# A hybrid layer in split fp32 on one core: the first block's keys take the DRAM round trip that the later blocks' keys take

## The chip, the core and the metric

One core of a Trainium2 chip runs the whole program. Its engines work side by side, each through its own queue in order: TensorE (PE: matrix products into PSUM; PEld are its weight loads), VectorE (DVE), ScalarE (ACT) and GpSimd (POOL) for elementwise work, and SyncE (SP), which here only issues DMAs. GpSimd issues DMAs too. The metric is device time in microseconds (us) of one execution; lower is better.

## What is computed

One layer over 2048 prompt tokens and 64 sample tokens. One wide projection gives the inputs of two paths: a short convolution (path A) and a gated linear recurrence over 8 heads in chunks of 64 tokens (path B, HGRN2). The two are gated, merged, projected and normalised, and a last gate adds a per-layer embedding. The part that the change touches is the recurrence:

```python
def hgrn2_block(S, q, k, v, logf):
    b = jnp.cumsum(logf, axis=1)
    ref = b[:, (L - 1) // 2][:, None]
    qe = q * jnp.exp(b - ref)
    ke = k * jnp.exp(ref - b)
    att = jnp.where(causal, jnp.einsum('bthk,bshk->bhts', qe, ke), 0.0)
    o = jnp.einsum('bhts,bshv->bthv', att, v) + jnp.einsum('bthk,bhkv->bthv', q * jnp.exp(b), S)
    b_last = b[:, -1]
    S_new = jnp.exp(b_last)[..., None] * S + jnp.einsum('bshk,bshv->bhkv', k * jnp.exp(b_last[:, None] - b), v)
    return S_new, o
...
fg = lb + (1.0 - lb) * jax.nn.sigmoid(f)
logf = jnp.log(fg)
kk = 1.0 - fg
qq = jax.nn.silu(q) * QK_SCALE
S_new, o = hgrn2_scan(S0, qq, kk, vv, logf)
o = o * lax.rsqrt(jnp.mean(o * o, axis=-1, keepdims=True) + EPS)
```

The last product of `S_new` sums over tokens, so both keys and values must stand with tokens on the partitions for it, while everything before it has features there.

## The kernel before

**Tiling.** The 2112 tokens are cut into three blocks of 768, 704 and 640 (the 64 sample tokens lie in the second). Activations lie with 128 features on the partitions and the block's tokens in the free direction. Every large product is done with fp32 values split into a high and a low part (`hi`, `lo`; line 225), three matmuls for one, and most of them by a Strassen scheme: `sgroup` makes a group of two weight columns from seven products of half the size, each product being 12 matmuls (lines 445 to 447) of half a block's tokens. Weights come from DRAM through the buffers `raw`, `hi`, `lo` and `s`; all other tiles (`r`) share a ring of 48 buffers.

**Path B.** `path_b` runs over the 8 heads. `head_prep` makes a head's gates, keys and values with one group of seven products, and its queries and output gate with another; a call-back in the middle of that second group, `scaled`, makes the keys (`ka` for a pair's first chunk, `kb` with both chunks scaled to the pair's end; lines 1004 to 1013). In the first block a third group (`gates`) follows for each head but the first.

**Steps between products.** The attention of a head does not run at once. `path_b` puts its steps into numbered slots, and `sgroup` calls one slot after each product (`hook`), so that they run between the products of the next head. `head_attn` is a generator with a step at each `yield`: the product of queries and keys (L1122, L1124; `p_a`), the product of keys and values (L1137; `p_u`, from which the states follow on VectorE, L1152), the output (L1175, L1177; `p_o`), and in the first block a separate scaling. Each block has two such generators for a head (four groups of 128 tokens, then the rest). `turn_o`, `read_o` and `scale_o` then bring the head's output back to features on partitions, and it is stored (`o`).

**Getting tokens on the partitions.** `turned` lets VectorE transpose 32x32 blocks (L1064) into a staging tile and writes it to DRAM on GpSimd's queue (L1066); `in_rows` reads it back in another order, also on GpSimd's queue (L1071). For values (`tv`) and outputs (`to`) the result is used as it lands; for keys (`tk`), GpSimd copies it once more so that a group's columns lie side by side (L1076). Before the change the first block does this for values and outputs only: its keys are transposed by TensorE against an identity (L1104) into PSUM, and ScalarE copies them out (L1106). Blocks two and three do it for keys as well. There `head_prep` asks for the reads in the order values, the output of the head before, keys; the list is put together afterwards with the keys in front.

**What sets the order.** A tile scheduler sorts the instructions of each engine by the order in which the code emits them, by hints (`issue_after`, `high_priority`, `behind_all`), and by when it reckons an operand to be ready. What stands on one engine's queue then runs strictly in that order. On GpSimd's queue a DMA is only issued; the queue goes on to the next instruction while it travels. An instruction that needs data which have not landed holds the queue.

Of the kernel before, what the change touches and what calls it, by code (L numbers as in the profile page):

```python
# [18 lines left out]
P = 128  # L19
# [75 lines left out]
def hybrid_step(  # L95
# [66 lines left out]
    def ps_attn():  # L162
        return psa.tile([P, 512], F32, tag="pa", name=nm("pa"))
# [74 lines left out]
    lows, turn, stores = {}, [0], [SP]  # L238
# [700 lines left out]
    def head_prep(bl, hc, hd, first, hs, before):  # L939
        n, npair, turn = bl["n"], bl["npair"], bl["turn"]  # L940
        nch = n // CH
        odd_end = turn > npair
        sf, vt = rt(), rt(turn * P)
        if odd_end:
            V.memset(vt[:, n - CH : n], 0.0)

        def sink_f(c, h, x, y):
            if c == 0:
                A.activation(half(sf, h), whole(x, y), AF.Sigmoid)
                return  # L950
            n1 = 0
            if h == 0:
                n1 = 2 * SWAP * CH
                for odd in range(2):
                    c3, to = (slice(o, 2 * SWAP, 2) for o in (odd, 1 - odd))
                    into(chunks(vt)[:, to, :], chunks(x[:, :n1])[:, c3, :], None if y is None else chunks(y[:, :n1])[:, c3, :])
            n2 = hn() - CH * (h and odd_end)
            into(half(vt, h)[:, n1:n2], x[:, n1:n2], None if y is None else y[:, n1:n2])
            if n2 < hn():
                into(vt[:, n : n + CH], x[:, n2:], None if y is None else y[:, n2:])  # L960

        if hs and hd == 0:
            plain_group(FF * 8, IV * 8, hs, sink_f)
        else:
            sgroup(FF * 8 + hd, IV * 8 + hd, hc, sink_f, first)
        lg, staged_k, eq, staged_v = rt(), rt(turn * P), rt(), rt(turn * P)
        b, qx = staged_k[:, :n], staged_v[:, :n]
        wrote = [turned("tv", vt, staged_v, turn)]
        A.activation(lg, sf, AF.Ln, bias=lb[:, hd : hd + 1], scale=omlb[:, hd : hd + 1])
        if not first:  # L970
            V.tensor_scalar(sf, sf, nomlb[:, hd : hd + 1], omlb[:, hd : hd + 1], ALU.mult, ALU.add)
        V.tensor_tensor_scan(b, keep[:, :n], lg, 0.0, ALU.mult, ALU.add)
        ref = chunks(b)[:, :, CH // 2 - 1 : CH // 2]
        V.tensor_tensor(chunks(lg), chunks(b), ref.to_broadcast([P, nch, CH]), ALU.subtract)
        qc = small.tile([P, 2, BN // CH], F32, tag="qc", name=nm("qc"))
        f, r = qc[:, 0, :nch], qc[:, 1, :nch]
        ka, kb, qe, z = hf(turn * CH), rt(turn * P), rt(), rt()

        def scaled(after):


            with tc.issue_after(after):
                if first:
                    A.activation(sf, sf, AF.Identity, bias=omlb[:, hd : hd + 1], scale=nomlb[:, hd : hd + 1])
                A.activation(r, ref.rearrange("p c o -> p (c o)"), AF.Exp)
                A.activation(eq, lg, AF.Exp)
                A.activation(lg, lg, AF.Exp, scale=-1.0)
            V.tensor_tensor(f[:, 1:nch], r[:, 1:nch], chunks(eq)[:, : nch - 1, CH - 1], ALU.mult)
            V.tensor_copy(f[:, 0:1], r[:, 0:1])
            for g in bl["groups"]:  # L990
                if g["sample"]:
                    c = g["off"] // CH
                    V.tensor_copy(f[:, c : c + 1], r[:, c : c + 1])
            f1, f2 = f[:, 0 : 2 * npair : 2], f[:, 1 : 2 * npair : 2]

            ka3 = ka.rearrange("p (g t) -> p g t", t=CH)
            more = turn - 2 * SWAP
            for lo, hi, to in (
                (0, SWAP, ka3[:, more + 1 :: 2, :]),
                (SWAP, 2 * SWAP, ka3[:, more : turn - 1 : 2, :]),  # L1000
                (2 * SWAP, turn, ka3[:, :more, :]),
            ):
                own = slice(2 * lo, min(2 * hi, nch), 2)
                V.tensor_tensor(to, chunks(sf)[:, own, :], chunks(lg)[:, own, :], ALU.mult)
                hi = min(hi, npair)
                scale = f2[:, lo:hi].unsqueeze(2).to_broadcast([P, hi - lo, CH])
                place = slice(2 * lo + (hi <= SWAP), 2 * hi, 2)
                V.tensor_tensor(chunks(kb)[:, place, :], to[:, : hi - lo, :], scale, ALU.mult)
            if odd_end:
                V.tensor_copy(chunks(kb)[:, nch - 1 : nch + 1, :], ka3[:, more - 1 : more, :].to_broadcast([P, 2, CH]))  # L1010
            for lo, hi in ((0, SWAP), (SWAP, npair)):
                seconds, place = slice(2 * lo + 1, 2 * hi, 2), slice(2 * lo + (hi > SWAP), 2 * hi, 2)
                V.tensor_tensor(chunks(kb)[:, place, :], chunks(sf)[:, seconds, :], chunks(lg)[:, seconds, :], ALU.mult)
            if not first:
                wrote.append(turned("tk", kb, staged_k, turn))
            V.tensor_tensor(f2, f2, f1, ALU.mult)

        def queries():
            if first:
                A.activation(qe, qe, AF.Silu)  # L1020
                V.scalar_tensor_tensor(qe, qe, QK_SCALE, eq, ALU.mult, ALU.mult)
            else:
                sq = rt()
                A.activation(sq, qe, AF.Sigmoid)
                V.scalar_tensor_tensor(qe, qe, QK_SCALE, sq, ALU.mult, ALU.mult)
                V.tensor_tensor(qe, qe, eq, ALU.mult)
            V.tensor_tensor(chunks(qx), chunks(qe), f.unsqueeze(2).to_broadcast([P, nch, CH]), ALU.mult)

        def sink_q(c, h, x, y):
            if c == 1:  # L1030
                into(half(qe, h), x, y)
            elif first:
                A.activation(half(z, h), whole(x, y), AF.Silu)
                A.mul(half(z, h), half(z, h), g_on[:, hd : hd + 1])
            else:
                v = whole(x, y)
                A.activation(half(z, h), v, AF.Sigmoid)
                V.scalar_tensor_tensor(half(z, h), v, g_on[:, hd : hd + 1], half(z, h), ALU.mult, ALU.mult)  # L1038

        with behind_all(summed[-1] if first and hd == 0 else ()):  # L1040
            sgroup(ZB * 8 + hd, QQ * 8 + hd, hc, sink_q, first, mid=scaled, free=first)
        with tc.issue_after(freed[0]) if first else nullcontext():
            queries()
        with behind_all([*wrote, *powers]):
            by_token = [in_rows("tv", turn)]
            if before is not None and not first:
                before["ot"] = in_rows("to", turn, before["on"])
            if not first:
                by_token.insert(0, in_rows("tk", turn))
        return dict(  # L1050
            eq=eq, f=f, ka=ka, kb=kb, qe=qe, qx=qx, vt=vt, z=z, by_token=by_token, on=None,
            npair=npair, turn=turn, more=turn - 2 * SWAP, first=first, last=bl["last"], carry=None,
        )
# [6 lines left out]
    def turned(kind, src, out, npair):  # L1060

        n = npair * P
        blocks4 = out[:, :n].rearrange("p (j g a) -> p g j a", j=4, a=32)
        V.transpose(blocks4, src[:, :n].rearrange("p (g b j) -> p g j b", b=32, j=4))  # L1064
        turning[kind] = dram.tile([P, n], F32, tag=f"{kind}{npair}", name=nm(kind), bufs=2)
        return G.dma_start(turning[kind], out[:, :n]).ins  # L1066
# [12 lines left out]
    def head_attn(ip, gs, d, hd):  # L1079
# [16 lines left out]

        ready = [t[:, o0 // P : o0 // P + nt] for t in d["by_token"]]
        if len(ready) == 1:  # L1100
            turn_ = ps_attn()
            with placed():
                for i, g in enumerate(gs):
                    T.transpose(turn_[:, i * P : i * P + P], cols(d["kb"], g), ident)  # L1104
            ready.insert(0, tile3())
            A.copy(ready[0], cols3(turn_, nt))  # L1106
        kt, v = ready
        p_a = ps_attn()
        with placed():
            for i, g in enumerate(gs):  # L1110
# [105 lines left out]
    def path_b(bl, hc, first, kept, fills, hs, lead_sums=None):  # L1216
# [9 lines left out]
        for hd in range(NH):  # L1226
# [11 lines left out]
            if first:  # L1238
                late = int(hd == 0)
                for g in attn:  # L1240
                    for slot in (1 + late, 4, 7, 10):
                        at(slot + late + (g is attn[1]), g)
                at(13 + late, partial(turn_o, d))
                at(17 + late, partial(read_o, d))
                at(24 + late, partial(scale_o, d), keep)
                for slot in (15, 17, 19) if hd else (17,):
                    at(slot, piece)
                if hd == NH - 1:
# [539 lines left out]
```

## Time and profile before

| | us |
|---|---|
| median of 3 runs (lowest, highest) | 2538.24 (2536.97, 2540.58) |
| the profiled execution | 2538.01 |
| its span, first to last instruction | 2536.1 |

The core's granted clock is 1.00 over the span. The times of the stages can be read from the rows of path B: the heads of the first block run from some 60 to 500 us, those of the second from 1060 to 1345, those of the third from 1860 to 2130.

How the rows below are read: a group's row names line, engine, operation, `out<-in` tiles and count; a row in order of time starts with its start and duration in us, and ends, where the engine sat idle before it, with that idle time and what ended it. A row of waits says who waited for whom: total us, times, longest us. A row of stretches gives start and end, the length, then the busy us of PE, PEld, DVE, ACT and POOL, each with its count, then TensorE's granted clock, the DMA engines' busy share and GB/s.

### The profile page before, as it was taken

How to read it: one execution, taken by the hardware profiler on the slowest of the kernel's cores; microseconds unless marked ns; L12 is line 12 of the kernel's file. 1: busy time of each engine (PE TensorE's matmuls, PEld its weight loads, DVE VectorE, ACT ScalarE, POOL GpSimd, SP SyncE). 2: the span in 40 equal slices, each digit the busy share in tenths (PEclk: the TensorE clock that was granted, in tenths of full speed). 3: DMA queues.
4: the chain of work that ended last, by engine and by line, in shares of the span. 5: the costliest groups of instructions: out<-in, count | busy, mean ns of one | idle time of the engine just before them, and what ended most of it. 6: DMA issues, size and time to landing. Idle time of an engine off the chain costs nothing. (4 is left out here: it accounts for less than half of the span.)

```text
span 2536.1 us, 46699 instructions
## 1 busy us (share of the span) xinstructions
PE 2518.9 (99%) x15982; PEld 2506.1 (99%) x15982; DVE 1841.7 (73%) x3593; ACT 1495.8 (59%) x2916; POOL 455.1 (18%) x801
## 2 busy tenths in 40 slices
PE   9999999999999999999999999999999999999999
PEld 9999999999999999999999999999999999999998
DVE  7889888898868775477775657978357775446967
ACT  6766676654453764466655556567356664455675
POOL 2012121221022021122222311102212221001111
PEclk9999999999999999999999999999999999999999
DMA  8789888997697888889989988989989988789986
GB/s 332 244 293 334 308 302 304 331 333 268 231 346 246 270 287 315 278 298 318 307 295 310 339 303 304 329 280 313 330 304 317 324 296 283 254 258 314 335 273 202
DMA packets 356334, 755.02 MB, mean 298 GB/s; under 512 B 44214, under 2 KB 49520, under 8 KB 356096
## 3 DMA queue, kind: packets, MB, share of 16 engines
q1 hardware_dynamic: 305856, 553.85, 64.1%
q0 software_dynamic: 50240, 198.19, 22.1%
q8 instruction: 126, 2.06, 0.3%
q14 instruction: 112, 0.92, 0.1%
HBM read 545.53 MB, written 206.33 MB: 296 GB/s over the span
## 5 line engine op out<-in xcount | busy, mean ns | idle before, releaser
L445 PE MATMUL pg<-r,hi 128*128 128x320 f32 (+2 forms) x3304 | 1075.5, 326 | 1.6 <-DVE r L1038 1.6
L446 PE MATMUL pg<-r,hi 128*128 128x320 f32 (+2 forms) x3304 | 1066.7, 323 | 0.0
L447 PE MATMUL pg<-r,lo 128*128 128x384 f32 (+2 forms) x2380 | 776.2, 326 | 0.0
L274 ACT CAST hi<-raw 128x512 fp32r<-128x512 f32 x658 | 405.2, 619 | 447.0 <-PE pg L446 182.4
L445 PEld LDWEIGHTS pg<-r,hi 128*128 128x128 f32 x3304 | 621.7, 188 | 2.1 <-ACT hf L459 1.8
L446 PEld LDWEIGHTS pg<-r,hi 128*128 128x128 f32 x3304 | 621.4, 188 | 0.0
L447 PEld LDWEIGHTS pg<-r,lo 128*128 128x128 f32 x2380 | 446.8, 188 | 0.5 <-DMA lo<-low 0.4
L225 ACT CAST hi<-raw 128x512 fp32r<-128x512 f32 x316 | 195.1, 620 | 187.3 <-PE pg L446 56.5
L447 PE MATMUL pg<-r,s 128*128 128x352 f32 (+1 forms) x924 | 292.3, 316 | 1.6 <-DMA s<-low 1.6
L597 PE MATMUL pg<-r,hi 128*128 128x320 f32 (+2 forms) x864 | 277.7, 322 | 0.3 <-DVE r L225 0.3
L596 PE MATMUL pg<-r,hi 128*128 128x320 f32 (+2 forms) x864 | 274.7, 322 | 0.0
L225 DVE TENSOR_TENSOR r<-r,r 128x320 fp32r<-128x320 f32 (+7 forms) x350 | 206.6, 608 | 41.5 <-ACT r L225 40.5
L225 DVE TENSOR_TENSOR lo<-raw,hi 128x512 fp32r<-128x512 f32 x263 | 179.8, 687 | 76.7 <-ACT hi L225 73.7
L225 ACT CAST r<-r 128x320 fp32r<-128x320 f32 (+7 forms) x350 | 183.7, 556 | 44.7 <-DVE r L393 9.1
L225 ACT CAST hi<-s 128x512 fp32r<-128x512 f32 x164 | 101.3, 619 | 142.1 <-PE pg L446 113.2
L598 PE MATMUL pg<-r,lo 128*128 128x352 f32 (+2 forms) x564 | 180.6, 321 | 0.4 <-DMA lo<-low 0.4
L447 PEld LDWEIGHTS pg<-r,s 128*128 128x128 f32 x924 | 173.5, 188 | 2.1 <-DMA s<-low 2.1
L635 PE MATMUL pg<-r,hi 128*128 128x384 f32 (+2 forms) x512 | 167.5, 328 | 0.2 <-DVE r L225 0.2
L634 PE MATMUL pg<-r,hi 128*128 128x384 f32 (+2 forms) x512 | 166.0, 328 | 0.2 <-ACT hi L274 0.2
L597 PEld LDWEIGHTS pg<-r,hi 128*128 128x128 f32 x864 | 162.1, 188 | 2.4 <-DVE r L225 1.8
L596 PEld LDWEIGHTS pg<-r,hi 128*128 128x128 f32 x864 | 161.3, 188 | 1.3 <-ACT r L225 0.8
L459 ACT COPY hf<-pg 128x352 f32<-128x352 f32 (+2 forms) x354 | 157.2, 446 | 0.7 <-PE pg L447 0.7
(385 smaller groups left out, 4139.0 us busy)
## 6 DMA issues: line engine op xcount, KB each, us to landing
raw<-w_blk SPq DMA_DIRECT2D x579, 256.0 KB, 4.5
raw<-S SPq DMA_DIRECT2D x436, 256.0 KB, 4.5
lo<-low SPq DMA_DIRECT2D x388, 256.0 KB, 4.3
s<-low SPq DMA_DIRECT2D x270, 256.0 KB, 4.7
low<-lo SPq DMA_DIRECT2D x239, 256.0 KB, 3.9
S<-s SPq DMA_DIRECT2D x152, 256.0 KB, 3.8
low<-r POOLq DMA_DIRECT2D x50, 256.0 KB, 4.8
r<-w_blk POOLq DMA_DIRECT2D x48, 256.0 KB, 7.1
```

Source lines behind the costliest of these rows:

```text
L225: return A.copy(hi, src).ins, V.tensor_tensor(lo, src, hi.bitcast(F32), ALU.subtract).ins
L274: A.copy(hi, raw)
L445: add(hi[:, k, :], xhi, start=start and k == 0, stop=False)
L446: add(hi[:, k, :], xlo, start=False, stop=False)
L447: last[0] = add(lo[:, k, :], xhi, start=False, stop=k == KH - 1).ins
L459: copied = A.copy(got[n], ps[bank])
L596: add(hi[:, k, :], xhi, start=start and k == 0, stop=False)
L597: add(hi[:, k, :], xlo, start=False, stop=False)
L598: last[0] = add(lo[:, k, :], xhi, start=False, stop=k == KH - 1).ins
L634: T.matmul(ps, hi[:, k % 4, :], xhi[:, c], start=k == ks[0], stop=False)
L635: T.matmul(ps, hi[:, k % 4, :], xlo[:, c], start=False, stop=False)
```

## The change

```diff
@@ head_prep, scaled
-            if not first:
-                wrote.append(turned("tk", kb, staged_k, turn))
+            wrote.append(turned("tk", kb, staged_k, turn))
             V.tensor_tensor(f2, f2, f1, ALU.mult)
@@ head_prep
         with behind_all([*wrote, *powers]):
-            by_token = [in_rows("tv", turn)]
+            by_token = [in_rows("tk", turn), in_rows("tv", turn)]
             if before is not None and not first:
                 before["ot"] = in_rows("to", turn, before["on"])
-            if not first:
-                by_token.insert(0, in_rows("tk", turn))
@@ head_attn
-        ready = [t[:, o0 // P : o0 // P + nt] for t in d["by_token"]]
-        if len(ready) == 1:
-            turn_ = ps_attn()
-            with placed():
-                for i, g in enumerate(gs):
-                    T.transpose(turn_[:, i * P : i * P + P], cols(d["kb"], g), ident)
-            ready.insert(0, tile3())
-            A.copy(ready[0], cols3(turn_, nt))
-        kt, v = ready
+        kt, v = (t[:, o0 // P : o0 // P + nt] for t in d["by_token"])
@@ path_b
             if first:
                 late = int(hd == 0)
                 for g in attn:
-                    for slot in (1 + late, 4, 7, 10):
+                    for slot in (1 + late, 6, 9, 12):
                         at(slot + late + (g is attn[1]), g)
-                at(13 + late, partial(turn_o, d))
-                at(17 + late, partial(read_o, d))
-                at(24 + late, partial(scale_o, d), keep)
+                at(15 + late, partial(turn_o, d))
+                at(19 + late, partial(read_o, d))
+                at(26 + late, partial(scale_o, d), keep)
```

The first block's keys are turned by VectorE, written, read back and copied by GpSimd like those of the other blocks. TensorE's transposes and ScalarE's copies of them are gone. In the first block every step of a head from `p_u` on stands two slots, so two products, later. The list of reads is built in one expression for all blocks, so `in_rows("tk")` is called ahead of `in_rows("tv")`. Lines after the change have lower numbers: L1122 is L1111, L1124 is L1113, L1137 is L1126, L1064 is L1061, L1066 is L1063, L1071 is L1068, L1076 is L1073.

TensorE, first head of the first block, at the product of queries and keys (`pa` is PSUM of the attention, `pg` that of the large products). Before:

```order
L447 MATMUL pg_1289<-r_813,lo_1217 128x384
L1104 MATMUL pa_1303<-ident,r_983 128x128 x4
L1122 MATMUL pa_1310<-r_984,hf_982 128x2x64
L1124 MATMUL pa_1310<-r_984,r_983 128x64
L1122 MATMUL pa_1310<-r_984,hf_982 128x2x64
L1124 MATMUL pa_1310<-r_984,r_983 128x64 x3
L445 MATMUL pg_1244<-r_582,hi_1222 128x384
```

And after:

```order
L447 MATMUL pg_1296<-r_813,lo_1224 128x384
L1111 MATMUL pa_1310<-r_984,hf_982 128x2x64
L1113 MATMUL pa_1310<-r_984,r_983 128x64
L1111 MATMUL pa_1310<-r_984,hf_982 128x2x64
L1113 MATMUL pa_1310<-r_984,r_983 128x64 x3
L445 MATMUL pg_1251<-r_582,hi_1229 128x384
```

The four transposes ahead of the product are gone, and the product stays where it was; the product of keys and values, further on, stands 24 matmuls (two products) later.

GpSimd, first block, from the first head's values to the second head's (`tv`, `tk`: the tiles in DRAM; `r<-tv`, `r<-tk`: the reads). Before:

```order
L1066 DMA tv_976<-r_974 128x768
L1071 DMA r_1174<-tv_976 128x4x192
L1066 DMA tv_1398<-r_1396 128x768
L692 TENSOR_TENSOR ms_1513<-ms_1513,mhalf 128x4
L692 TENSOR_TENSOR ms_1555<-ms_1555,mhalf 128x2
```

And after:

```order
L1063 DMA tv_976<-r_974 128x768
L1063 DMA tk_1112<-r_972 128x768
L1068 DMA r_1177<-tk_1112 128x4x192
L1073 COPY r_1179<-r_1177 128x768
L1068 DMA r_1181<-tv_976 128x4x192
L1063 DMA tv_1375<-r_1373 128x768
```

The keys' write, read and copy are new, and the values' read has moved from ahead of them to behind the copy.

GpSimd, second block, second head, between its keys' write and the next head's values. Before:

```order
L1066 DMA to_13679<-r_13135 128x768
L1066 DMA tk_13647<-r_13502 128x768
L1071 DMA r_13717<-tv_13506 128x4x192
L1071 DMA r_13598<-to_13679 128x4x192
L1071 DMA r_13720<-tk_13647 128x4x192
L1076 COPY r_13722<-r_13720 128x768
L1066 DMA tv_13916<-r_13914 128x768
```

And after:

```order
L1063 DMA to_13639<-r_13095 128x768
L1063 DMA tk_13607<-r_13462 128x768
L1068 DMA r_13558<-to_13639 128x4x192
L1068 DMA r_13677<-tk_13607 128x4x192
L1073 COPY r_13679<-r_13677 128x768
L1068 DMA r_13681<-tv_13466 128x4x192
L1063 DMA tv_13876<-r_13874 128x768
```

The same instructions stand there, but the read of the values has moved from right behind the keys' write to behind the copy of the keys. The third block's queue changed in the same way.

## The prediction

> **What bounds the kernel now.** I read the profile in this order: the page's busy times, the table of who TensorE waited for, then GpSimd's queue in order of time at the heads of each block.
>
> ```profile
> span 2536.1 us, 46699 instructions
> PE 2518.9 (99%) x15982; PEld 2506.1 (99%) x15982; DVE 1841.7 (73%) x3593; ACT 1495.8 (59%) x2916; POOL 455.1 (18%) x801
> ...
> PE pa L703 <- POOL cols L692: 2.9, 5, 0.8
> PE pg L447 <- DMA s<-low: 1.6, 1, 1.6
> ...
> PE pa L1137 <- POOL r L1076: 0.8, 1, 0.8
> ```
>
> TensorE is busy for 99% of the span, and the table (total us, times, longest) lists only some ten microseconds of waits. So whatever leaves TensorE is a gain, whatever makes it wait is a loss, and the other engines count only through such waits. The last row is the one to keep: at L1137, the product of keys and values, TensorE already waits once for GpSimd's copy of the keys. That copy happens in the second and third blocks, where the keys already take the DRAM round trip. This is how GpSimd's queue looks there, for one head of each block, with the product that uses the result:
>
> ```profile
> 1114.68 0.54 POOL L1066 DMA_DIRECT2D tk<-r  x1 [4.33 <-DVE r L1064]
> 1115.21 0.77 POOL L1071 DMA_DIRECT2D r<-tv  x1
> 1115.98 0.76 POOL L1071 DMA_DIRECT2D r<-to  x1
> 1120.11 0.75 POOL L1071 DMA_DIRECT2D r<-tk  x1 [3.37 <-DMA tk<-r]
> 1127.49 0.82 POOL L1076 COPY r<-r 128x768 f32<-128x768 f32 x1 [6.63 <-DMA r<-tk]
> ...
> 1129.07 1.50 PE L1137 MATMUL pa<-r,r 128*128 128x128 f32 x12
> ...
> 1937.17 0.54 POOL L1066 DMA_DIRECT2D tk<-r  x1 [3.25 <-DVE r L1064]
> ...
> 1943.08 0.75 POOL L1071 DMA_DIRECT2D r<-tk  x1 [3.86 <-DMA tk<-r]
> 1950.09 0.72 POOL L1076 COPY r<-r 128x640 f32<-128x640 f32 x1 [6.26 <-DMA r<-tk]
> ...
> 1950.86 1.38 PE L1137 MATMUL pa<-r,r 128*128 128x128 f32 x10
> ```
>
> Columns are start and duration in us. The copy stands in GpSimd's queue and waits 6 us for the read of the keys; nothing behind it in the queue goes out meanwhile. It ends at 1128.31 and 1950.81; the product starts 0.8 and 0.05 us later. The values' read (r<-tv) went out before all that and costs nothing today.
>
> **Part 1: 48 transposes leave TensorE.**
>
> ```profile
> L1104 PE MATMUL pa<-ident,r x48: 270/272/273, 98.5 to 454.3; 128*128 128x128 f32 x48
> ...
> 98.51 0.60 PE L1104 MATMUL pa<-ident,r 128*128 128x128 f32 x4
> 98.95 0.39 PE L1122 MATMUL pa<-r,hf 128*128 128x128 f32 x2
> ```
>
> Four start 0.44 us before the next product, so one takes 0.11 us of the queue: 48 x 0.11 = 5.3 us less. The 16 ScalarE copies behind them go too; as the table has no ScalarE wait in this stage, that is worth nothing more.
>
> **Part 2: the round trip in the first block.** For the first head:
>
> ```profile
> 89.68 0.62 DVE L1013 TENSOR_TENSOR r<-r,r 128x128 f32<-128x128 f32 x2
> 90.76 0.69 DVE L225 TENSOR_TENSOR lo<-s,hi 128x512 fp32r<-128x512 f32 x1
> ...
> 76.95 1.55 DVE L1064 STREAM_TRANSPOSE r<-r 128x768 f32<-128x768 f32 x1
> 78.80 0.57 POOL L1066 DMA_DIRECT2D tv<-r  x1 [15.17 <-DVE r L1064]
> 82.36 0.78 POOL L1071 DMA_DIRECT2D r<-tv  x1 [2.99 <-DMA tv<-r]
> ...
> 105.64 1.05 PE L1137 MATMUL pa<-r,r 128*128 128x128 f32 x8
> ...
> DMA to landing us min/median/max: 3.7/5.0/7.3
> ```
>
> The order puts the keys' transpose behind the L225 that ends at 91.45. It takes 1.55 us (93.0); 0.3 us later the write goes out (93.3), and a read can follow 3.56 us after a write, as at 78.80 and 82.36 (96.9). The last row holds all such reads of this block, median 5.0: 101.9. The copy, 0.1 + 0.8: 102.8. Only then does the values' read go out, since it now stands behind the copy: 0.1 + 5.0, 107.9. The product came at 105.64; without six transposes (0.66) and 24 matmuls later (0.175 each, 4.2) it comes at 109.2. At the median nothing waits; with two reads of 7.3 it waits 3.3, with two of 3.7 not at all. I take 0.5 us. Heads two to eight have far more room:
>
> ```profile
> 124.82 0.42 DVE L1013 TENSOR_TENSOR r<-r,r 128x256 f32<-128x256 f32 x1
> ...
> 154.35 0.49 PE L1137 MATMUL pa<-r,r 128*128 128x128 f32 x3
> ...
> 160.00:210.00 50.00, 50.00 (x308) 49.69 (x307) 44.96 (x86) 35.58 (x74) 10.09 (x16) 1.00 0.84 299
> ```
>
> In the second head, keys are ready at 125.2 and used at 154.4, 29 us later, and the chain above takes 17. The last row is a stretch of about one head (length; then busy us of PE, PEld, DVE, ACT, POOL; clock, DMA share): VectorE has 5.0 us free and gets 1.6 more, GpSimd 40 free and gets a copy of 0.8 and two issues. That free time and the weights split ahead of use hide it: 0. If that cover fails, at most 8 x 1.6 = 13 us come on top; a gain is excluded, as TensorE waits for nothing here. The steps moved by two products issue what they issued before; the output's write (to) and read move with them and stand behind the copy and the values' read on GpSimd, some us later. The output is used seven products after its read's place (7 x 2.1 = 15 us), which covers that.
>
> **Part 3: the later blocks' queue.** The new list names the keys' read first and the values' second for every block, and the scheduler follows: in blocks two and three r<-tv drops from ahead of the keys' read to behind the copy. Behind the copy means behind the keys' write, read and copy, in order. The values, not the keys, are then late at the product. TensorE takes its queue in order too, so all products behind L1137 wait. The chain starts from the keys' write, whose distance to the product does not change: 1129.07 - 1114.68 = 14.4 us in block two, 1950.86 - 1937.17 = 13.7 in block three. Its durations:
>
> ```profile
> tk<-r POOLq DMA_DIRECT2D x8, 384.0 KB, 4.3
> r<-tk POOLq DMA_DIRECT2D x8, 384.0 KB, 7.4
> tk<-r POOLq DMA_DIRECT2D x8, 320.0 KB, 5.3
> r<-tk POOLq DMA_DIRECT2D x8, 320.0 KB, 6.8
> ...
> DMA to landing us min/median/max: 4.3/4.3/4.3
> ...
> DMA to landing us min/median/max: 4.5/4.5/4.5
> ...
> DMA to landing us min/median/max: 2.6/5.8/8.7
> ...
> DMA to landing us min/median/max: 3.1/6.1/7.5
> ```
>
> The first four are medians from issue to landing. The next two are reads of the same size with no other head transfer beside them, the last of each block. The last two hold all writes and reads of the keys in blocks two and three. No row shows the values' read alone in the middle of these blocks, so it lies between 4.4 (alone) and 7.4 (three together). The keys' read keeps one neighbour of two: I take 6.2, the middle of 7.4 and the first block's 5.0. The values' read has only the weights beside it: 5.6, between 5.0 and 6.2. The write loses a neighbour: 4.1 and 5.0.
>
> Block two: 4.1 + 0.3 to the issue + 6.2 + 0.1 + 0.8 copy + 0.1 + 5.6 + 0.1 = 17.3, less 14.4: TensorE waits 2.9 us. Block three: 5.0 + 0.3 + 6.2 + 0.1 + 0.7 + 0.1 + 5.6 + 0.1 = 18.1, less 13.7: 4.4 us. Eight heads each: 23.2 + 35.2 = 58.4. The last head of a block has the short write (2.6 and 3.1): 1.5 and 1.9 less, so 55.0. Bounds: with reads of 4.4, 14.3 and 15.1, so 0 and 1.4, together 11; with the medians of today (7.4 and 6.8, writes 4.3 and 5.3), 20.5 and 20.2, so 6.1 and 6.5, together 98 after the last heads. The wait does not pile up: each head's chain starts from TensorE's own progress. It is not won back either, as TensorE is the bound.
>
> **The sum.** The profiled run took 2538.0 us (span 2536.1 and 1.9 around it), 0.2 below the median of the three. 2538.0 - 5.3 + 0.5 + 55.0 = 2588 us. With the bounds of part 3: 2544 and 2631.
>
> **Rivals.**
> *The reads are quick.* With both reads at 4.8, the sums are 15.1 and 15.9, the waits 0.7 and 2.2: 23 us, less 3 for the last heads, so 2554. For it: the lone reads. Against it: those fell after the heads' work, and the keys' read, which mostly runs after its neighbours have landed, still takes 6.8 to 7.4.
>
> *The clock falls in the pauses.*
>
> ```profile
> 1.13 5.04 PE L177 MATMUL pa<-hf 128*128 128x128 f32 x22 [1.13 <-DVE hf L174]
> ...
> 2531.31 0.31 PE L636 MATMUL pg<-r,lo 128*128 128x320 f32 x1
> ...
> 2530.00:2535.00 5.00, 1.61 (x12) 1.35 (x10) 0.99 (x2) 0.44 (x1) 0.00 (x0) 1.00 0.18 66
> 2535.00:2536.10 1.10, 0.00 (x0) 0.00 (x0) 0.00 (x0) 0.00 (x0) 0.00 (x0) 0.63 0.00 0
> ```
>
> After idling, TensorE began at 0.23 us per pass (5.04 / 22), half of the 0.11 above, for some 5 us. At the end the granted clock was 1.00 until 2535 and 0.63 on average after it; if the fall is to a half, it came 0.3 us in, 3.7 us after the last matmul. Pauses of 4.4 us in block three could do that and cost 2.5 us each for seven heads: 17 us, so 2605; with the reads of today's medians and a fall in 14 pauses, 2631 + 35 = 2666. Against it: the pauses forecast for block two are under 3.7, and the longest of today (1.6) shows no fall.
> [...]
>
> *The values come in time.* If two reads together take under 8.9 us in block two and under 7.4 in block three, L1137 waits for nothing, the transposes' 5.3 us are all that is left, and the time is 2533, faster. It decides at those sums. For it: the first block's shortest read, 3.7. Against it: even two lone reads (4.3 + 4.5) make 8.8, and no head of block three could be so quick throughout. It is also the case if the change did only what its words say, but the order shows otherwise.
>
> *VectorE is late in the first block*, with up to 13 us: 2601.
>
> **Chances.** The forecast (waits of 2 to 4.5 us per head, 2570 to 2605): 0.55. Quick reads: 0.18. Falling clock, or reads at today's medians (above 2605): 0.21. Values in time: 0.04. VectorE late: 0.02. The range from 2553 to 2626 leaves out the rest on both sides. About 0.2% is what a measurement of this kernel can tell from no change; faster by more than that 0.03 (5.3 us is 0.21%, just over), within it 0.02, slower 0.95.
>
> **What would show it.** Right: L1104 is gone; the table of TensorE's waits has the keys-times-values product waiting for r<-tv some 16 times, 55 us in total, none in the first block beyond a few us; on GpSimd r<-tv starts right after the copy; the reads beside it take 5 to 6.5 us. Wrong: the waits end with the copy and not with r<-tv (the keys are late); or the product waits in the first block's later heads, or weights (lo, hi) are named there; or a granted clock under 1.00 in blocks two and three. If both reads land within 4.5 us, the size is wrong and not the mechanism.

## The result and the profile after

| | before | after |
|---|---|---|
| median of 5 runs, us | 2538.24 | 2651.7 (2647.31 to 2654.57) |
| ratio | 1 | 1.0439, 95% interval [1.0426, 1.0452] |
| span of the profiled execution, us | 2536.1 | 2647.0 |
| mean granted clock over the span | 1.00 | 0.982 |

The changed kernel is slower by 113 us; 50 were forecast. The page's first lines for the changed kernel:

```profile
span 2647.0 us, 46640 instructions
PE 2553.4 (96%) x15934; PEld 2535.0 (96%) x15934; DVE 1855.0 (70%) x3601; ACT 1487.9 (56%) x2900; POOL 482.9 (18%) x825
```

TensorE is busy for longer, though the change took 48 transposes from it. A busy time that grows (2518.9 us before) while the work shrinks points to a slower clock. The table of TensorE's waits (who waits for whom: us in total, times, longest):

```profile
PE pa L1126 <- DMA r<-tv: 67.9, 16, 6.3
PE pg L445 <- ACT hi L225: 7.0, 2, 4.2
...
PE pg L447 <- DMA s<-low: 1.5, 2, 0.8
PE pg L447 <- DMA lo<-low: 1.3, 2, 1.0
PE pg L447 <- DVE lo L225: 1.3, 2, 0.7
```

L1126 is the product of keys and values (L1137 before). It now waits for the values 16 times, once per head of blocks two and three, as forecast. The rows below it, for weights of the large products, were not. Those for `hi` and for `lo` from VectorE lie in the first block, where before had no such wait; those for `low` lie later, and of their kind before had one wait of 1.6 us. Now the stretches of the same trace (start, end, length, then busy us and count of PE, PEld, DVE, ACT, POOL, then granted clock, DMA share, GB/s):

```profile
60.00:500.00 440.00, 431.38 (x2585) 428.32 (x2584) 381.03 (x704) 284.48 (x586) 111.70 (x163) 0.99 0.88 307
...
1095.00:1400.00 305.00, 272.02 (x1707) 269.91 (x1706) 187.88 (x444) 152.42 (x259) 61.96 (x94) 0.93 0.76 253
...
1945.00:2225.00 280.00, 243.08 (x1626) 240.73 (x1625) 163.65 (x379) 144.44 (x253) 56.33 (x85) 0.92 0.75 255
```

The granted clock is 0.93 and 0.92 in the heads of blocks two and three. The trace's records of the clock hold 1.00 or 0.50 and no other value, so that is 2 x 0.07 x 305 = 43 us and 2 x 0.08 x 280 = 45 us at half clock. The stretches between them stayed at 1.00.

One head of block two shows the mechanism. GpSimd's queue in order of time, then the product on TensorE:

```profile
1133.49 0.54 POOL L1063 DMA_DIRECT2D tk<-r  x1 [4.33 <-DVE r L1061]
1134.02 0.77 POOL L1068 DMA_DIRECT2D r<-to  x1
1139.08 0.76 POOL L1068 DMA_DIRECT2D r<-tk  x1 [4.28 <-DMA tk<-r]
1146.08 0.82 POOL L1073 COPY r<-r 128x768 f32<-128x768 f32 x1 [6.24 <-DMA r<-tk]
1146.85 0.75 POOL L1068 DMA_DIRECT2D r<-tv  x1
```
```profile
1152.15 2.60 PE L1126 MATMUL pa<-r,r 128*128 128x128 f32 x12 [3.77 <-DMA r<-tv]
```

The copy stands 6.24 us in the queue, waiting for the keys' read. The values' read leaves right behind it, at 1146.85, and the product starts 5.3 us later, after TensorE has idled for 3.77 us. Its 12 passes take 2.60 us, 0.22 each, where the trace of before had 12 in 1.50. The same place in steps of one microsecond (PE busy and count, granted clock, DMA share, GB/s):

```profile
1151.00:1152.00 1.00, 0.00 (x0) 1.00 0.99 369
1152.00:1153.00 1.00, 0.85 (x5) 0.74 0.22 82
1153.00:1154.00 1.00, 1.00 (x7) 0.50 0.00 0
1154.00:1155.00 1.00, 1.00 (x6) 0.50 0.00 0
1155.00:1156.00 1.00, 1.00 (x6) 0.56 0.03 8
1156.00:1157.00 1.00, 1.00 (x8) 1.00 0.00 0
```

In this head the clock falls to a half when the pause is over and the work has begun, and stays there for 0.52 + 2 + 0.88 = 3.4 us. So the pause is paid twice: once as idle time, and again as half-speed work. Of the 16 pauses 14 had a fall, three of them like this one. The other 11 falls begin 0.7 to 2.9 us before the pause ends and last 6.8 us, as in this row, where the pause ends at 1351.62 and the clock is already at a half with TensorE idle:

```profile
1350.60:1351.60 1.00, 0.00 (x0) 0.01 (x1) 0.00 (x0) 0.00 (x0) 0.00 (x0) 0.50 0.34 122
```

Added up fall by fall, 85 us of the two stretches are at half clock (the 88 above come from rounded clocks). Of these, 17 lie inside the pauses and cost nothing more, and under the other 68 I take half of the speed as lost, an estimate: 34 us. With the 67.9 us of waits that makes 102 us.

**The first block** lost time as well. Here are a place on GpSimd's queue in the trace of before, and the same place after, where `r<-w_blk` are the weights that are split ahead for the later blocks:

```profile
222.30 0.77 POOL L1071 DMA_DIRECT2D r<-tv  x1
223.06 2.14 POOL L382 DMA_DIRECT2D r<-w_blk  x4
```
```profile
231.52 0.77 POOL L1068 DMA_DIRECT2D r<-tk  x1 [0.68 <-PE pg L447]
238.23 3.28 POOL L1073 COPY r<-r 128x768 f32<-128x768 f32 x1 [5.93 <-DMA r<-tk]
241.46 0.76 POOL L1068 DMA_DIRECT2D r<-tv  x1
242.22 0.56 POOL L1063 DMA_DIRECT2D to<-r  x1
242.76 1.60 POOL L382 DMA_DIRECT2D r<-w_blk  x3
```

The weights' reads went out at 223.06; now they stand behind the copy and go out from 242.76 on. Who waits for them shows on the line of those reads:

```profile
who waited for it (us, times):
  ACT r L225: 21.1, 2
```

ScalarE takes its queue in order as well. Twice it stood for some ten microseconds at the cast of those weights (before, this row is missing), and the casts `hi` that TensorE needed stood behind it. These are the two waits for `hi`. Around them the clock fell too:

```profile
250.00:260.00 10.00, 6.54 (x29) 6.09 (x29) 7.92 (x15) 6.21 (x12) 2.71 (x5) 0.83 0.98 354
352.00:362.00 10.00, 6.18 (x27) 5.88 (x28) 6.72 (x12) 5.90 (x10) 2.93 (x5) 0.66 0.92 354
```

That is 3.4 and 6.8 us at half clock, of which 2.1 lie inside the second wait.

### The profile page after: what moved, and what is told of

Same layout as the page of the kernel before. It is cut to its first block, busy times and chain, and to the rows that moved or that the text cites. A ratio compares the mean times of both kernels' runs of the same rounds, so it can differ in the third digit from the quotient of the medians.

```text
span 2647.0 us, 46640 instructions
## 1 busy us (share of the span) xinstructions
PE 2553.4 (96%) x15934; PEld 2535.0 (96%) x15934; DVE 1855.0 (70%) x3601; ACT 1487.9 (56%) x2900; POOL 482.9 (18%) x825
## 3 DMA queue, kind: packets, MB, share of 16 engines
q0 software_dynamic: 51776, 204.48, 21.7%
## 4 chain that ended last, share of the span: by engine, by line
PE 64%; DMA 10%; issue 9%; DVE 5%; POOL 2%; ACT 0%; SPq 0%; POOLq 0%; DVEq 0%; ACTq 0%
PE pg L447 13%; PE pg L445 13%; PE pg L446 13%; PE pg L596 4%; PE pg L597 4%; PE pg L598 4%; DMA r<-tv 3%; PE pg L636 3%; PE pg L635 3%; PE pg L634 3%; DMA r<-tk 2%; DMA tk<-r 2%; PE pa L1126 2%; DMA low<-lo 1%; DMA lo<-low 1%
## 5 line engine op out<-in xcount | busy, mean ns | idle before, releaser
L445 PE MATMUL pg<-r,hi 128*128 128x320 f32 (+2 forms) x3304 | 1085.6, 329 | 7.9 <-ACT hi L225 7.0
L445 PEld LDWEIGHTS pg<-r,hi 128*128 128x128 f32 x3304 | 630.0, 191 | 8.9 <-ACT hi L225 7.4
L446 PEld LDWEIGHTS pg<-r,hi 128*128 128x128 f32 x3304 | 629.4, 190 | 0.0
L447 PEld LDWEIGHTS pg<-r,lo 128*128 128x128 f32 x2380 | 453.8, 191 | 5.6 <-DVE lo L225 3.1
L597 PEld LDWEIGHTS pg<-r,hi 128*128 128x128 f32 x864 | 162.1, 188 | 1.6 <-DVE r L225 0.9
L596 PEld LDWEIGHTS pg<-r,hi 128*128 128x128 f32 x864 | 161.3, 188 | 1.3 <-ACT r L225 0.8
```

What stands on the lines that cost most here:

```text
L445: add(hi[:, k, :], xhi, start=start and k == 0, stop=False)
L446: add(hi[:, k, :], xlo, start=False, stop=False)
L447: last[0] = add(lo[:, k, :], xhi, start=False, stop=k == KH - 1).ins
L596: add(hi[:, k, :], xhi, start=start and k == 0, stop=False)
L597: add(hi[:, k, :], xlo, start=False, stop=False)
```

## Experiments

**x1: the old order in blocks two and three only.** The first block keeps the change.

```diff
-            by_token = [in_rows("tk", turn), in_rows("tv", turn)]
+            by_token = [in_rows("tk" if first else "tv", turn)]
             if before is not None and not first:
                 before["ot"] = in_rows("to", turn, before["on"])
+            by_token.insert(first, in_rows("tv" if first else "tk", turn))
```

> The first block keeps the change; blocks two and three read values, output, keys in that order again, as before the change. Theory Q (in the later blocks only the place of the values' read on GpSimd's queue costs, by waits of TensorE and the half clock that follows them): the two stretches lose their 51 and 50 us, so 2651.7 - 101 = 2551 us, 2546 to 2556, no wait for r<-tv at the keys-times-values product, granted clock 1.00 from 500 us on. Rival R (something else that the change does costs there, such as tiles or GpSimd's copies in the first block that the later blocks inherit): 2600 or more. What is left over 2538 is then the price of the first block alone: some 9.5 us by the comparison of TensorE's progress, against the forecast's gain of 5.

Measured: 2549.87 us, ratio to before 1.004 [1.0025, 1.0055]. No wait for `r<-tv` is left, and the clock of both stretches is back at 1.00. So the order of the reads in the later blocks costs 2651.7 - 2549.9 = 102 us, and the first block costs the other 9.0 (2549.87 - 2540.89, the median of before on that chip). Theory Q holds.

**x2: the other half alone.** The kernel before, with the keys' read asked for first in blocks two and three.

```diff
-            by_token = [in_rows("tv", turn)]
+            by_token = [] if first else [in_rows("tk", turn)]
+            by_token.append(in_rows("tv", turn))
             if before is not None and not first:
                 before["ot"] = in_rows("to", turn, before["on"])
-            if not first:
-                by_token.insert(0, in_rows("tk", turn))
```

> The kernel before, with its first block untouched; only blocks two and three read keys, values, output. Theory Q: 16 waits for r<-tv of 4.2 us and some 33 us at half clock, 2538 + 101 = 2639 us, 2631 to 2647. If only waits counted (the forecast's own price): 2538 + 55 to 68 = 2593 to 2606. Rival R: within 5 us of 2538.

Measured: 2634.05 us, 1.0371 [1.0352, 1.039], so 93 us. The table of waits has:

```profile
PE pa L1137 <- DMA r<-tv: 62.7, 16, 6.0
```

One reordered list, with the first block untouched, makes most of the loss. The waits alone, 63 us, do not reach the 93; the trace has 79 us at half clock in these blocks (the stretches' clocks are 0.94 and 0.93), 15 of them inside the waits, which adds 64 / 2 = 32 us and makes 95.

**x3: the pauses filled.** Throwaway products keep TensorE busy while it would wait.

```diff
         p_u = ps_attn()
         with placed():
+            for _ in range(0 if d["first"] or o0 else 24):
+                T.matmul(p_u[:, :P], ident, ident, start=True, stop=True)
             for i in range(nt):
```

> The changed kernel with 24 throwaway products of the identity with itself on TensorE right ahead of each first keys-times-values product of blocks two and three (24 x 0.11 = 2.6 us, inside the mean wait of 4.2 us; their results are overwritten). Nothing else moves. Theory C (the fall of the clock is a second price of each pause, paid only when the array is idle): the waits named shrink from 68 to 68 - 42 = 26 us, the granted clock of the two stretches goes from 0.76 and 0.75 of the DMA-and-clock rows' 0.93 and 0.92 to 1.00, and the time falls by the 33 us at half clock: 2619 us, 2612 to 2628. Rival W (the pauses are all of it; half clock only fills time that would be waited anyway): 2648 to 2655. Rival F (the throwaway products are not inside the wait but come on top): 2652 + 42 = 2694.

(In the expectation, 0.76 and 0.75 are the DMA shares of the rows above; the clocks meant are 0.93 and 0.92.) Measured: 2638.64 us, 1.0388 [1.0371, 1.0406]: more work, and 13 us less than the changed kernel. The waits and the two stretches:

```profile
PE pa L1126 <- DMA r<-tv: 3.6, 5, 1.1
```
```profile
1095.00:1400.00 305.00, 303.92 (x2137) 303.76 (x2136) 192.18 (x452) 157.11 (x266) 62.99 (x96) 1.00 0.78 259
...
1945.00:2225.00 280.00, 275.19 (x2042) 274.01 (x2041) 167.07 (x383) 147.55 (x259) 57.95 (x87) 1.00 0.77 257
```

The clock stays at 1.00, but the time fell by less than the 33 us forecast, since the products were costed wrongly. Each takes two passes: the trace has 768 passes, 48 at each of 16 places. At 0.11 us a pass they take 84.5 us, more than the pauses they fill. With that, 2651.7 - 67.9 of waits + 3.6 left + 84.5 - H = 2638.6 gives H = 33 us for the half clock. That agrees with the 34 us counted above. Without a price for the clock the run would have come to 2672.

**y1: half as many.** The same edit with 12 products, 2.6 us, which fit inside the mean wait.

```diff
-            for _ in range(0 if d["first"] or o0 else 24):
+            for _ in range(0 if d["first"] or o0 else 12):
```

> As x3, with 12 throwaway products in place of 24. The trace of x3 shows that each is two passes (768 rows in 32 places, the second group of a head too), so 24 of them took 5.3 us or more, longer than the mean wait of 4.2; 12 take 2.6 to 2.7 us. Theory C (half clock is a price of its own, paid when the array idles): the waits of 68 us shrink by 16 x 2.7 to 25, the second group of each head adds 16 x 2.7 = 43 us that no wait covers, the 33 us at half clock are gone: 2651.7 - 33 + 43 = 2662 us, granted clock 1.00 in both stretches. Rival W (only the waits count, half clock is free): 2651.7 + 43 = 2695. For comparison x3 by the same sum: 16 x 5.4 = 86 us on the second groups and 86 in place of the 68 of waits: 2651.7 - 33 - 68 + 4 + 172 = 2727 by C; it measured 2639, so either the second groups ran no such products or the count is by pass; if by pass, with one place per head, x3 by C is 2651.7 - 33 - 68 + 4 + 85 = 2640, and this run 2651.7 - 33 = 2619.

The trace has 24 passes at each of 16 places, so the last case of that text is the one that holds: 2619 us by theory C, and by W, where half clock is free, as much as the changed kernel, 2652. Measured: 2628.01 us, 1.0363 [1.034, 1.0385], nearer to C and not at it. The rows say why:

```profile
PE pa L1126 <- DMA r<-tv: 27.6, 13, 3.3
```
```profile
1095.00:1400.00 305.00, 294.73 (x1993) 293.76 (x1992) 194.89 (x457) 160.11 (x274) 65.94 (x102) 0.99 0.79 267
...
1945.00:2225.00 280.00, 264.07 (x1878) 262.61 (x1877) 171.56 (x391) 151.53 (x267) 58.20 (x88) 0.98 0.78 264
```

The rest of each pause, up to 3.3 us, still let the clock fall in five heads: 2 x (0.01 x 305 + 0.02 x 280) = 17 us at half clock, 9 us lost, and 2619 + 9 = 2628.

**x4: values first in all blocks.**

```diff
-            by_token = [in_rows("tk", turn), in_rows("tv", turn)]
+            by_token = [in_rows("tv", turn)]
             if before is not None and not first:
                 before["ot"] = in_rows("to", turn, before["on"])
+            by_token.insert(0, in_rows("tk", turn))
```

> The changed kernel, with values, output, keys as the order of reads in all three blocks. Theory Q: blocks two and three as in x1. In the first block the weights that are split ahead (r<-w_blk) still stand behind the copy of the keys on GpSimd's queue, which still waits for the keys' read: if that wait (theory G) is what the first block loses, the time equals x1 within 3 us, 2548 to 2554. If instead the late values' read was what the first block lost (rival V), 2533 to 2540, at or below the kernel before.

Measured: 2553.09 us, 1.0051 [1.0036, 1.0066]. In the first block it does not matter which read is asked for first: the loss is that of x1 (2549.87 us; the intervals overlap). The copy still holds the queue ahead of the weights' reads (theory G); rival V falls.

**y2: the first block's copy later.** x1, with the copy issued by the step that makes the product of queries and keys.

```diff
-            by_token = [in_rows("tk" if first else "tv", turn)]
+            by_token = [in_rows("tk" if first else "tv", turn, late=first)]
...
-    def in_rows(kind, npair, t=None):
+    def in_rows(kind, npair, t=None, late=False):
...
-        kt = rt(npair * P)
-        G.tensor_copy(kt.rearrange("q (g i a) -> q g i a", i=4, a=32), t)
-        return cols3(kt, npair)
+        def side_by_side():
+            kt = rt(npair * P)
+            G.tensor_copy(kt.rearrange("q (g i a) -> q g i a", i=4, a=32), t)
+            return cols3(kt, npair)
+        return side_by_side if late else side_by_side()
...
+        if callable(d["by_token"][0]):
+            d["by_token"][0] = d["by_token"][0]()
```

> x1 with one thing more: in the first block GpSimd's copy of the keys is issued with the step of the queries-times-keys product (two products after the reads) and no longer right behind the keys' read, so that the values' read and the weights' reads (r<-w_blk) do not stand behind it. Theory G (the first block's loss comes from those weights: late reads, ScalarE's in-order split of them, TensorE's two pauses of 3 to 5 us and the half clock behind each): the two pauses near 250 and 350 us go, the 5 us of the transposes come out: 2533 us, 2530 to 2538. Rival S (the loss comes from the steps moved by two products or VectorE's 24 more transposes): 2545 or more.

Measured: 2539.76 us, 1.001 [1.0, 1.0019]. The place shown above, on GpSimd's queue:

```profile
228.88 0.77 POOL L1067 DMA_DIRECT2D r<-tk  x1 [0.67 <-DMA tk<-r]
229.64 0.76 POOL L1067 DMA_DIRECT2D r<-tv  x1
230.39 0.55 POOL L382 DMA_DIRECT2D r<-w_blk  x1
...
246.17 0.84 POOL L1073 COPY r<-r 128x768 f32<-128x768 f32 x1
```

All reads go out at once, and the copy no longer waits. ScalarE's wait for the weights fell from 21.7 us in x1 to 9.7, and the loss against before on the same chip from 9.0 to 1.2 us. The traces show it in the first block: at 500 us x1's TensorE is 10.3 us behind the kernel before (by the starts of the same product), y2's is 1.8 ahead. One wait for `hi`, of 2.6 us near 341 us, is left; the weights' read still goes out 7 us later than before (230.39 against 223.06). Theory G holds for the mechanism, though the 2533 us that it named were not reached: at 1500 us the same TensorE is 4.1 us behind. One place on the way is a wait of 2.2 us near 1352 us with a fall of the clock behind it (0.99 from 1095 to 1400); the rest of that loss stays open.

**y3: the weights' reads on another queue.** x1, with `SP.dma_start(t, w_blk[i, h])` in place of `G.dma_start` at L382.

> x1 with one thing more: the weights that are split ahead (r<-w_blk) are read on SP's queue, so that GpSimd's queue cannot hold them. Theory G: 2533 us as y2, unless SP's queue, which waits for free weight buffers, gives them out later than GpSimd did, or shifts other weights behind them: then some pauses named lo<-low, hi or s stay, up to 2550. Rival S: 2545 or more, with the w_blk reads landing before their split is reached and the pauses still there.

Measured: 2550.87 us, 1.0059 [1.0042, 1.0076], as slow as x1. The two waits for `hi` of x1 (7.5 us) are gone, but SP's queue carries all other weights, and others took their place (one for ScalarE's `r` of 2.8 us, three for VectorE's states of 1.9 together). Moving the reads to a full queue is no cure. It tells less than y2 does, since it changes the order of that queue too, and its trace is of the fastest of four executions (2544.94 us), 6 us below the median.

**y4: the moved steps alone**, on the kernel before.

```diff
-                    for slot in (1 + late, 4, 7, 10):
+                    for slot in (1 + late, 6, 9, 12):
...
-                at(13 + late, partial(turn_o, d))
-                at(17 + late, partial(read_o, d))
-                at(24 + late, partial(scale_o, d), keep)
+                at(15 + late, partial(turn_o, d))
+                at(19 + late, partial(read_o, d))
+                at(26 + late, partial(scale_o, d), keep)
```

> The kernel before, with only the steps of the first block's heads moved as in the change (keys-times-values, output, scaling and the output's round trip two products later). Theory G: nothing, 2538 us, 2535 to 2541. Rival S (the move itself costs in the first block): 2545 or more.

Measured: 2540.80 us, 1.0012 [1.0003, 1.0022], between 0.8 and 5.6 us slower. No wait of the first block explains it (its trace is 0.8 us behind at 500 us), so I leave open whether the move costs two or three microseconds; it is not the 9 of x1.

**z1: the changed order kept, the copy late in all blocks.** y2's edit with `late=True` everywhere, and the reads in the change's order.

```diff
+            by_token = [in_rows("tk", turn, late=True), in_rows("tv", turn)]
```

> The changed kernel with its order of reads kept (keys, then values, then the output of the head before where it is asked for), but GpSimd's copy of the keys issued in all three blocks with the step of the queries-times-keys product, so that it no longer stands between the two reads. Theory H (it is the copy, which waits in GpSimd's queue for the keys' read, that holds the values back; the order of the two reads by itself costs little): r<-tv goes out 0.8 us behind r<-tk, both land before the product or within 1 to 2 us of it, 2540 to 2558 us, the table names at most a few waits for r<-tv or the copy, 15 us in all. Rival O (whatever is read second comes too late, since the two reads and the output's travel one after the other): waits for r<-tv or r<-tk of 2 us or more at all 16 heads, 2590 or more.

Measured: 2547.16 us, 1.0037 [1.0022, 1.0053]. The waits of TensorE and the queue in block two:

```profile
PE pa L1126 <- DMA r<-tv: 6.2, 9, 1.9
```
```profile
1122.85 0.76 POOL L1067 DMA_DIRECT2D r<-tk  x1 [4.88 <-DMA tk<-r]
1123.60 0.75 POOL L1067 DMA_DIRECT2D r<-tv  x1
1129.65 0.82 POOL L1073 COPY r<-r 128x768 f32<-128x768 f32 x1 [5.30 <-DMA r<-tk]
```

This is the sharpest of the runs. The keys are still read first, and yet the waits for the values fall from 67.9 to 6.2 us and none of them reaches 2. It was not the order of two reads that cost the 102 us, but the copy between them, waiting in the queue. What is left, 7.6 us above before where y2 had 1.2, puts what the order by itself still costs at some 6 us; in the trace nearly all of it arises behind the first block (TensorE is 1.2 us behind at 500 us).

**z2 and z3: the weights read one and two pieces earlier**, on top of y2, for a version that beats both kernels. The diff is that of z2; z3 has the new line one sum earlier.

```diff
+            nxt = load(firsts[n + 1]) if pieces and n + 1 < len(firsts) else nxt
             keep("S4", i1, a12, a12, a11, ALU.subtract)
...
-                nxt = load(firsts[n + 1])
                 yield
```

> y2 with one thing more: the weights split ahead in the first block (r<-w_blk) are read one piece earlier, with the step that makes the sum before the last, so that the reads of keys and values do not stand right ahead of them where their split is near. Theory G: the remaining pauses of y2 near 340 us (2.6 and 2.2 us, ScalarE waiting 6.4 us for r<-w_blk) go, 2540 - 5 = 2535 us, 2532 to 2539. Rival: the ring's four tiles, taken earlier, are missing elsewhere, 2542 or more.

> As z2, with the read two pieces earlier. Theory G: as z2, 2532 to 2539, and the lower of the two if any split still waits for r<-w_blk in z2. Rival: tiles missing elsewhere, 2542 or more.

Measured: z2 2539.01 us, 0.9998 [0.9989, 1.0007]; z3 2540.81 us, 1.0008 [0.9999, 1.0018]. ScalarE's wait for these weights is down to 0.8 us in z2. At 500 us its TensorE is 3.9 us ahead of the kernel before (the starts of the same product in both traces), so the transposes' 5.3 us do come out in the first block. They were not kept: at the end of the span z2 is level. One of the places is a wait that the kernel before has too (L445 at 2091 us, 1.6 us in its table of waits, 2.0 in that of z2); z2's row, and then that of before:

```profile
2085.00:2100.00 15.00, 12.81 (x80) 12.18 (x79) 10.00 (x20) 7.20 (x14) 3.65 (x5) 0.89 0.87 281
```
```profile
2085.00:2100.00 15.00, 12.34 (x87) 11.84 (x86) 12.64 (x27) 6.17 (x13) 3.54 (x5) 1.00 0.80 264
```

In z2 the clock fell there, in before it did not. Whether z2 is a little faster or not at all stays open: its interval runs from 2.8 us faster to 1.8 slower.

## Why the prediction was wrong

The direction, the place and the mechanism of the main loss were right; its price was too low, and a second place was called free.

- **Part 1, transposes, 5.3 us less:** borne out as far as it can be seen, by z2's lead of 3.9 us after the first block.
- **Part 2, first head, 0.5 us:** right within that half microsecond. The values' read left at 103.75 (forecast 102.9) and the product started at 109.69 (109.2), with no wait for them.
- **Part 2, "That free time and the weights split ahead hide it: 0":** this step failed. I counted the free time of GpSimd and VectorE, 40 and 5.0 us per head, and not what stands behind a waiting copy. The weights split ahead, which I named as cover, were the victims: their reads stand behind the copy, ScalarE's queue behind their cast, and TensorE behind ScalarE. x1 puts the first block at +9.0 us in place of -4.8. The trace of x1 adds up to it: 9.2 us of waits in the first block, where before had none, plus half of the 10.1 us at half clock outside these waits, less the 5.3, make 8.9. That the swing of 14 us lies near the 13 that I allowed for a failed cover is luck: those were for VectorE's transposes, and 7.5 of the 9.2 us are waits for ScalarE's `hi`.
- **Part 3, the waits, 55.0 us:** mis-sized by 13, nearly all of it in block two: 33.0 us where 21.7 were forecast, against 34.9 and 33.3 in block three. The durations that came (medians from issue to landing; write, keys' read, values' read, of block two and then block three):

```profile
tk<-r POOLq DMA_DIRECT2D x8, 384.0 KB, 4.7
r<-tk POOLq DMA_DIRECT2D x8, 384.0 KB, 6.7
r<-tv POOLq DMA_DIRECT2D x8, 384.0 KB, 5.7
...
tk<-r POOLq DMA_DIRECT2D x8, 320.0 KB, 4.7
r<-tk POOLq DMA_DIRECT2D x8, 320.0 KB, 6.5
r<-tv POOLq DMA_DIRECT2D x8, 320.0 KB, 5.5
```

  With them the same sum gives 4.7 + 0.3 + 6.7 + 0.1 + 0.8 + 0.1 + 5.7 + 0.1 - 14.4 = 4.1 us, and 4.3 in block three, where 2.9 and 4.4 were forecast. I took 6.2 for the keys' read and 4.1 for block two's write. The first seven heads of each block waited 4.5 and 4.8 us in the mean. The deduction for the last heads was right in kind and too small: they waited 1.2 and 1.1 us, over 3 less than the others, where 1.5 and 1.9 were taken off.
- **The price of a pause:** the larger error, 33 us. The forecast's sum took a pause to cost its own length. The profile of before held the row that said otherwise, the clock of 0.63 at the span's end, and I used it for a rival at 0.21 ("Pauses of 4.4 us in block three could do that and cost 2.5 us each"). What I held against it was that the pauses of block two lie under 3.7 us, as if 3.7 were a threshold. x3 gives 33 / 16 = 2.1 us for each pause. All 14 pauses of 3.6 us or more had a fall, at 34 / 14 = 2.4 us each, near the 2.5 of that rival; the two of the last heads had none. The rival with "reads of today's medians and a fall in 14 pauses", 2666, came nearest, in part by luck: its 98 us of waits were 30 too many, and its first block was a gain.

Together: 13 + 33 = 46 of the 47 us by which the later blocks missed (102 against 55), and 14 in the first block. Of the signs that the prediction named for being wrong, two came: `hi` and `lo` in the table of waits, and a clock under 1.00 in blocks two and three.

## What to carry to other kernels

On an in-order queue the question is not whether an engine has time, but what stands behind an instruction that waits; put a copy that waits for a transfer behind the issues that do not, as y2 and z1 did. Follow each instruction that it holds to who needs it next, through every in-order queue on the way. And where TensorE is the bound, a pause of a few microseconds costs more than its length: price it with the half clock that follows, 2 us per pause here, and prefer many short waits to a long one (with those of z1, up to 1.9 us, the clock of the stretches stayed at 0.99 to 1.00).

## What the runs showed of the hardware

**The clock needs less than a long pause to fall.** In z1 the waits at L1126 reach 1.9 us and the clock of the stretches stays at 0.99 to 1.00; in z2 a wait of 2.0 us in the row at 2085 is followed by 2 x 0.11 x 15 = 3.3 us at half clock; in y4 one of 2.2 us at the same product is not (1.00 from 2085 to 2100). In the changed kernel 14 of the 16 pauses (4.2 us in the mean) had a fall, of 3.4 us or twice that. All falls within its trace begin and end on one grid with steps of 3.41 us, save the last, which the trace's end cuts. In the head shown above, TensorE is busy for 0.32 us of the step from 1149.06 to 1152.47, at a clock of 1.00; the next step, busy throughout, is at 0.50, and the one behind it at 1.00 again. Idle time by the records of TensorE, counted per step of this grid over the changed kernel's trace (without the ends of the span), shows the same everywhere. At full clock, all 16 steps with 2.1 us or more of idle time were followed by a step at half clock, and none of the other 727, which have 1.2 us at most. At half clock, the next step stayed there when 0.68 us or more were idle (12 of 12) and came back to full after a step without idle time (16 of 16). So in this trace the idle time within a step goes with the fall. That the waits of z2 and y4 fared differently because they lay differently on such steps is my estimate from it; no row shows it.

**GpSimd's copy is slower in the first block.** The same copy of 128x768 values, in the first block and then in blocks two and three of the changed kernel (min, median, max in ns):

```profile
L1073 POOL COPY r<-r x8: 1058/1452/3277, 102.7 to 449.6; 128x768 f32<-128x768 f32 x8
```
```profile
L1073 POOL COPY r<-r x16: 713/770/825, 1105.0 to 2208.4; 128x768 f32<-128x768 f32 x8, 128x640 f32<-128x640 f32 x8
```

In the slowest case, 238.2 to 241.5, VectorE is busy for all 3.30 us, with seven operations. No run here took VectorE's work away, so whether that made the copy slow is not shown.
